# A block of two transformer layers on one core: wide and narrow matmuls in turns, and modulation columns in buffers of their own

## The chip, the cores and the metric

One core of a Trainium2 chip. TensorE (PE in the profile; PEld is its weight load), VectorE (DVE), ScalarE (ACT) and SyncE (SP, which only issues DMAs here) share one on-chip memory. The metric is the time of one execution on the device in microseconds (us), lower is better. A matmul here has a 128 x 128 weight tile and 512 ("wide") or 256 ("narrow") columns.

## What is computed

Two transformer blocks on x of 256 tokens by 2048 features, batch 1, in float32. Cut to what the change touches:

```python
def first_block(x, c, w_ada, b_ada, ...):
    mod = silu(c) @ w_ada + b_ada                   # 2048 -> 6 * 2048
    sh1, sc1, gt1, sh2, sc2, gt2 = split(mod, 6)
    h = rms_norm(x, g_mix) * (1 + sc1) + sh1
    z = h @ w_in            # q, k, v of two attentions, an indexer, two gates
    o_sb = stick_breaking_attention(...)            # 8 heads
    o_ds = indexer_sparse_attention(...)            # 8 heads, top 64 of 256 keys
    merged = sigmoid(gate_sb) * (o_sb @ w_o_sb) + sigmoid(gate_ds) * (o_ds @ w_o_dsa)
    x = x + gt1 * (merged @ w_out)
    h = rms_norm(x, g_ffn) * (1 + sc2) + sh2
    x = x + gt2 * ((silu(conv3(h @ w_gate)) * (h @ w_up)) @ w_down)
    return rms_norm(x, g_final)

def second_block(x, ...):     # gated linear attention, then a SwiGLU network
```

The second block has no modulation. Weights of all layers come from memory once, 583 MB in all.

## The kernel before

**Splitting.** Every weight tile of 128 x 1024 float32 (512 KB) is fetched by `weights` into a buffer `raw`, rounded by ACT into `hi` (L96), and DVE writes the rest, raw minus hi, into `lo` (L97). Activations are held as hi and lo halves too, side by side in a 512-column slot. A product is hi times (hi, lo) plus lo times hi. There are seven `raw`, four `hi` and four `lo` buffers, so the split runs up to four tiles ahead of PE.

**The matmul forms.** `dense_b` and `dense_wide` (most of the run) use a pair for each 128 x 128 tile: one wide matmul of `hi` with both halves (L114), then one narrow matmul of `lo` with the hi half (L115), both added into one accumulator bank. `mm3` (batches of the first projection, `dense_3`) uses three narrow ones (L124 to L126); `dense_a` uses three wide ones (L167 to L169), with the roles of weight and activation exchanged.

**Modulation.** Each of the 96 columns of `mod` is a 128 x 2048 slice (1 MB) of `w_ada`, multiplied with silu(c) and summed by DVE. `mod_fetch` takes two `raw` buffers for it, two DMAs of 512 KB (L201); `mod_reduce` does two DVE reductions of 1024 (L211), the second starting from the first's sum. The first 32 columns (shift and scale of the first norm) are needed one by one in `batch`, which runs the first projection for three groups of outputs over k = 0, 1, then 2 to 6, then 7 to 15. The other 64 are paced: `weights` adds `rate` to a credit at each tile and calls `mod_step` (reduce the oldest, then fetch the next) when it reaches one. 48 of them have to be there when `ffn` starts.

**The order of stages.** First projection (`batch`, to about 320 us), values of both attentions (`values`, `dense_a`), gate projections by `dense_3` with the attention's small steps taken from a list `bg` one per tile by `pump` (about 430 to 630 us), the two output projections, `w_out`, then the feed-forward network, the second block and its SwiGLU. A norm ends in `stat_end`: sums over features by PE, `keep_warm` (matmuls of ones whose result nobody reads), a square root.

**Who sets the order.** The program is written as one sequence; a scheduler orders each engine's instructions from the dependencies, the buffers and a priority (`high_priority(offset=120)` moves fetch and split ahead). All loads stand in SP's queue in one order: a load that waits for its buffer holds those behind it.

## Time and profile before

| what | value |
|---|---|
| median of 3 runs | 2732.74 us (2729.59 to 2732.83) |
| profiled execution | 2736.31 us |
| its span, first to last instruction | 2734.5 us, mean granted clock 0.997 |
| PE busy | 2684.6 us, 98% |
| DVE busy | 1879.9 us, 69% |
| ACT busy | 1299.8 us, 48% |
| read from memory | 579 MB, 213 GB/s over the span |

A busy PE says that matmuls follow one another, not that they follow at the smallest distance: matmul records overlap, and the distance from one start to the next is what counts. The granted clock is 1.00 at 2.4 GHz and 0.50 at 1.2 GHz.

### The profile page before, as it was taken

What the parts mean: (1) busy time and instruction counts of PE and PEld (TensorE: products, weight loads), DVE (VectorE), ACT (ScalarE), POOL (GpSimd) and SP (SyncE); (2) the same over time, 40 slices, a digit from 0 to 9 for tenths busy, and PEclk for the clock granted to TensorE, in tenths of its full rate; (3) what the DMA queues carried; (4) which work ended last, traced back from release to release, by engine and by line L of the source; (5) the groups of instructions that cost most, each with busy time, mean ns of one, the idle gap of its engine ahead of it and who ended that gap; (6) DMA issues with size and microseconds to landing.
All of it is one profiled execution on the core that took longest, in us unless ns stands there. A gap on an engine that the chain in (4) does not pass through costs nothing.

```text
span 2734.5 us, 42023 instructions
## 1 busy us (share of the span) xinstructions
PE 2684.6 (98%) x16364; PEld 2375.6 (87%) x16364; DVE 1879.9 (69%) x2892; ACT 1299.8 (48%) x1925; POOL 0.2 (0%) x4
## 2 busy tenths in 40 slices
PE   8999998999989999999999999999999999999999
PEld 7999878999878888888888888888888888888888
DVE  7997686667888777766555578467766666665544
ACT  5343344554445444444444465455544444444333
POOL 0000000000000000000000000000000000000000
PEclk9999999999999999999999999999999999999999
DMA  9998778678767666655666545545555555556664
GB/s 338 333 358 292 265 234 295 223 245 283 264 226 231 219 232 224 225 186 185 181 185 189 189 137 147 167 148 186 191 175 187 186 185 186 187 187 184 196 193 124
DMA packets 167681, 585.71 MB, mean 214 GB/s; under 512 B 18583, under 2 KB 23415, under 8 KB 167481
## 3 DMA queue, kind: packets, MB, share of 16 engines
q1 hardware_dynamic: 167482, 583.03, 65.0%
q8 instruction: 128, 2.10, 0.3%
q14 instruction: 71, 0.58, 0.1%
HBM read 579.22 MB, written 3.67 MB: 213 GB/s over the span
## 4 chain that ended last, share of the span: by engine, by line
PE 79%; DVE 5%; DMA 5%; issue 1%; ACT 0%; SPq 0%; DVEq 0%; ACTq 0%
PE acc L114 43%; PE acc L115 22%; DMA raw<-in_w_ada 3%; DVE lo L97 3%; PE acc L125 2%; PE acc L124 2%; PE acc L126 2%; PE acc L167 1%; PE acc L168 1%; PE acc L169 1%; PE misc L868 1%; PE acc L149 1%; DMA skew<-t 1%; DVE raw L211 0%; DMA raw<-in_w_in_b 0%
## 5 line engine op out<-in xcount | busy, mean ns | idle before, releaser
L114 PE MATMUL acc<-slot,hi 128*128 128x512 f32 x5024 | 1777.5, 397 | 0.0
L97 DVE TENSOR_TENSOR lo<-raw,hi 128x1024 fp32r<-128x1024 f32 (+1 forms) x916 | 1101.4, 1205 | 653.1 <-ACT hi L96 652.1
L96 ACT CAST hi<-raw 128x1024 fp32r<-128x1024 f32 (+1 forms) x916 | 946.1, 1034 | 1191.0 <-issue 483.7
L115 PE MATMUL acc<-slot,lo 128*128 128x256 f32 x5024 | 1415.7, 282 | 6.8 <-DVE lo L97 6.8
L114 PEld LDWEIGHTS acc<-slot,hi 128*128 128x128 f32 x5024 | 943.2, 188 | 231.5 <-issue 1.5
L115 PEld LDWEIGHTS acc<-slot,lo 128*128 128x128 f32 x5024 | 947.0, 188 | 9.7 <-DVE lo L97 8.7
L124 PE MATMUL acc<-slot,hi 128*128 128x256 f32 x1056 | 301.3, 286 | 6.5 <-ACT hi L96 3.5
L126 PE MATMUL acc<-slot,lo 128*128 128x256 f32 x1056 | 297.7, 284 | 8.7 <-DVE lo L97 8.7
L125 PE MATMUL acc<-slot,hi 128*128 128x256 f32 x1056 | 297.6, 283 | 0.0
L126 PEld LDWEIGHTS acc<-slot,lo 128*128 128x128 f32 x1056 | 200.0, 190 | 10.7 <-DVE lo L97 10.6
L124 PEld LDWEIGHTS acc<-slot,hi 128*128 128x128 f32 x1056 | 200.4, 190 | 8.2 <-ACT hi L96 4.5
L125 PEld LDWEIGHTS acc<-slot,hi 128*128 128x128 f32 x1056 | 200.7, 190 | 0.0
L211 DVE CUSTOM_DVE_ANT_0 raw<-raw,big,vecs 128x1024 f32<-128x1024 f32 x96 | 123.0, 1282 | 101.5 <-DMA raw<-in_w_ada 101.3
L211 DVE CUSTOM_DVE_ANT_0 raw<-raw,big,mod 128x1024 f32<-128x1024 f32 x96 | 123.0, 1281 | 8.8 <-DMA raw<-in_w_ada 8.0
L124 PE MATMUL misc<-slot,hi 128*128 128x256 f32 x384 | 105.7, 284 | 1.8 <-ACT hi L96 1.4
L125 PE MATMUL misc<-slot,hi 128*128 128x256 f32 x384 | 105.0, 282 | 0.0
L167 PE MATMUL acc<-hi,slot 128*128 128x512 f32 x256 | 103.2, 403 | 1.4 <-DVE slot L578 1.4
L126 PE MATMUL misc<-slot,lo 128*128 128x256 f32 x384 | 97.5, 286 | 5.1 <-DVE lo L97 4.7
L168 PE MATMUL acc<-lo,slot 128*128 128x512 f32 x256 | 101.3, 396 | 0.0
L169 PE MATMUL acc<-hi,slot 128*128 128x512 f32 x256 | 101.2, 395 | 0.0
L179 DVE TENSOR_TENSOR t<-acc,t 128x256 f32<-128x256 f32 x188 | 78.6, 418 | 0.3
L178 ACT COPY t<-acc 128x256 f32<-128x256 f32 x209 | 76.3, 365 | 0.8 <-PE acc L150 0.8
(228 smaller groups left out, 1792.4 us busy)
## 6 DMA issues: line engine op xcount, KB each, us to landing
raw<-in_w_gu SPq DMA_DIRECT2D x344, 512.0 KB, 3.9
raw<-in_w_ada SPq DMA_DIRECT2D x192, 512.0 KB, 5.5
raw<-in_w_in_k SPq DMA_DIRECT2D x96, 512.0 KB, 5.8
raw<-in_w_down SPq DMA_DIRECT2D x80, 512.0 KB, 3.6
raw<-in_w_dn SPq DMA_DIRECT2D x80, 512.0 KB, 3.7
raw<-in_gla_b SPq DMA_DIRECT2D x66, 512.0 KB, 3.5
raw<-in_w_in_b SPq DMA_DIRECT2D x50, 512.0 KB, 5.4
raw<-in_w_in_a SPq DMA_DIRECT2D x32, 512.0 KB, 4.5
```

The lines of the kernel that those rows point to most:

```text
L96: self.mark = nc.scalar.copy(hi[:, :n], raw[:, :n])
L97: nc.vector.tensor_sub(lo[:, :n], raw[:, :n], hi[:, :n])
L114: nc.tensor.matmul(acc, hi[:, w], x, start=(k + j == 0), stop=False, skip_group_check=True)
L115: nc.tensor.matmul(acc[:, 1], lo[:, w], x[:, 0], start=False, stop=(k + j == kt - 1), skip_group_check=True)
L124: nc.tensor.matmul(out, hi, x[:, 0], start=first, stop=False, **mm)
L125: nc.tensor.matmul(out, hi, x[:, 1], start=False, stop=False, **mm)
L126: nc.tensor.matmul(out, lo, x[:, 0], start=False, stop=last, **mm)
L167: nc.tensor.matmul(o, hs[k][:, 0, tt], hi[:, w], start=(k == 0), stop=False)
L168: nc.tensor.matmul(o, hs[k][:, 0, tt], lo[:, w], start=False, stop=False)
L169: nc.tensor.matmul(o, hs[k][:, 1, tt], hi[:, w], start=False, stop=(k == KD - 1))
L179: nc.vector.tensor_add(out, acc[:, 0], t)
L211: nc.vector.tensor_tensor_reduce(out=raw, in0=raw, in1=self.c_act[:, hf * 1024:(hf + 1) * 1024], scale=1.0, scalar=init, op0=ALU.mult, op1 ...
```

## The change

- `tile_mm` takes the place of the pair in `dense_b` and `dense_wide`: in each four tiles the first two are wide then narrow, the other two narrow then wide.
- A column of `w_ada` is one DMA of 1 MB into a tile `col` with two buffers of its own, and one DVE reduction over 2048. `raw` has four buffers in place of seven, the small scratch `t1` six in place of seven.
- `mod_step` fetches first and reduces the column before, so a column is fetched one step ahead. `batch` fetches at other places, and takes columns while more than one is waiting.
- `rate` is set by stage: 0.25, 0.2, 0.15, 0.38, 0.33, 0.25 in place of 0.28 throughout.
- In the list `bg` the first sparse-attention head's second step comes after two empty entries, so two weight tiles (48 matmuls) later.
- `keep_warm` in `stat_end` has 20 matmuls in place of 12.

```diff
--- before.py
+++ after.py
@@ -64,7 +64,7 @@
 
     def scr(self, n):
         if n <= S:
-            return self.sp.tile([P, S], F32, name="t1", tag="t1", bufs=7)
+            return self.sp.tile([P, S], F32, name="t1", tag="t1", bufs=6)
         return self.sp.tile([P, 512], F32, name="t2", tag="t2", bufs=4)[:, :n]
 
     def acc(self):
@@ -84,7 +84,7 @@
 
 
     def raw(self):
-        return self.wp.tile([P, 1024], F32, name="raw", tag="raw", bufs=7)
+        return self.wp.tile([P, 1024], F32, name="raw", tag="raw", bufs=4)
 
     def weights(self, src, n):
         nc = self.nc
@@ -101,8 +101,21 @@
             self.mod_step()
         return hi, lo
 
+    def tile_mm(self, acc, hi, lo, x, j, first, last):
+
+        def wide(start, stop):
+            self.nc.tensor.matmul(acc, hi, x, start=start, stop=stop, skip_group_check=True)
+
+        def narrow(stop):
+            self.nc.tensor.matmul(acc[:, 1], lo, x[:, 0], start=False, stop=stop, skip_group_check=True)
+        if j % 4 < 2 or first:
+            wide(first, False)
+            narrow(last)
+        else:
+            narrow(False)
+            wide(False, last)
+
     def dense_b(self, src, kt, hs, evac, pump=0):
-        nc = self.nc
         acc = self.acc()
         k = 0
         while k < kt:
@@ -110,10 +123,7 @@
             hi, lo = self.weights(src[:, k * P:(k + kn) * P], kn * P)
             for j in range(kn):
                 w = slice(j * P, (j + 1) * P)
-                x = hs[k + j]
-                nc.tensor.matmul(acc, hi[:, w], x, start=(k + j == 0), stop=False, skip_group_check=True)
-                nc.tensor.matmul(acc[:, 1], lo[:, w], x[:, 0], start=False, stop=(k + j == kt - 1),
-                                 skip_group_check=True)
+                self.tile_mm(acc, hi[:, w], lo[:, w], hs[k + j], j, k + j == 0, k + j == kt - 1)
             k += kn
             self.pump(pump)
         evac(acc)
@@ -145,10 +155,7 @@
             for j in range(8):
                 k, acc = k0 + j // nn, accs[j % nn]
                 w = slice(j * P, (j + 1) * P)
-                x = hs[k]
-                nc.tensor.matmul(acc, hi[:, w], x, start=(k == 0), stop=False, skip_group_check=True)
-                nc.tensor.matmul(acc[:, 1], lo[:, w], x[:, 0], start=False, stop=(k == kt - 1),
-                                 skip_group_check=True)
+                self.tile_mm(acc, hi[:, w], lo[:, w], hs[k], j, k == 0, k == kt - 1)
             self.pump(pump)
         for acc, evac in zip(accs, evacs):
             evac(acc)
@@ -194,28 +201,23 @@
         if not self.modq:
             return
         ci, j = self.modq.popleft()
-        raws = []
         with self.tc.high_priority(offset=offset):
-            for hf in range(2):
-                raws.append(self.raw())
-                self.nc.sync.dma_start(raws[-1], self.ap["w_ada"][ci * KD + j, :, hf * 1024:(hf + 1) * 1024])
-        self.colq.append((ci, j, raws))
+            col = self.wp.tile([P, D], F32, name="col", tag="col", bufs=2)
+            self.nc.sync.dma_start(col, self.ap["w_ada"][ci * KD + j])
+        self.colq.append((ci, j, col))
 
     def mod_reduce(self):
-        nc = self.nc
-        ci, j, raws = self.colq.popleft()
+        ci, j, col = self.colq.popleft()
         n = ci * KD + j
-        m = self.mod[ci][:, j:j + 1]
-        for hf, raw in enumerate(raws):
-            init = m if hf else self.vec["b_ada"][:, n:n + 1]
-            nc.vector.tensor_tensor_reduce(out=raw, in0=raw, in1=self.c_act[:, hf * 1024:(hf + 1) * 1024], scale=1.0,
-                                           scalar=init, op0=ALU.mult, op1=ALU.add, accum_out=m)
+        self.nc.vector.tensor_tensor_reduce(out=col, in0=col, in1=self.c_act, scale=1.0,
+                                            scalar=self.vec["b_ada"][:, n:n + 1], op0=ALU.mult, op1=ALU.add,
+                                            accum_out=self.mod[ci][:, j:j + 1])
         return ci, j
 
     def mod_step(self):
-        if self.colq:
+        self.mod_fetch()
+        if self.colq and (len(self.colq) > 1 or not self.modq):
             self.mod_reduce()
-        self.mod_fetch()
 
 
     def stat_begin(self, two=False):
@@ -269,7 +271,7 @@
         r1, r2 = self.rs[:, :S], self.rs[:, S:]
         if not self.st_two:
             self.token_sums(m[:, :S], (self.st[:, :S], self.sq[:, :S]))
-            self.keep_warm(12)
+            self.keep_warm(20)
             self.free(self.st)
             self.rstd(r1, m[:, :S], D)
             return r1
@@ -564,11 +566,11 @@
                         w = slice(j * P, (j + 1) * P)
                         self.mm3(banks[n // 2][:, (n % 2) * S:(n % 2 + 1) * S], hi[:, w], lo[:, w], hs[k],
                                  k == k0 and n % 2 == 0, k == k1 - 1)
-                    if len(hss) < KD:
-                        for _ in range((0, 3)[half] if b == k == 0 else 1 - half):
+                    for _ in range((0, 2)[half] if b == k == 0 else 1 if k == 0 else half):
+                        while len(self.colq) > 1:
+                            column()
+                        if len(hss) < KD:
                             self.mod_fetch()
-                if len(hss) < KD:
-                    column()
             for n in range(KD):
                 o, sc = dst[b * KD + n]
                 a = banks[n // 2][:, (n % 2) * S:(n % 2 + 1) * S]
@@ -586,7 +588,7 @@
         with self.tc.issue_after(self.mark.ins):
             nc.scalar.preload_act_table_set("natural_log_exp_and_others")
         self.load_consts()
-        self.rate = 0.28
+        self.rate = 0.25
         self.modq.extend((ci, j) for ci in (2, 4, 3, 5) for j in range(KD))
         batch(1, 7, KD)
         batch(2, 7, KD)
@@ -618,10 +620,11 @@
                 out.append(v)
             return out
 
+        self.rate = 0.2
         self.dsv = values(0, 2)
         parts = [self.ds_head(h) for h in range(NH)]
-        self.bg.append(parts[0][0])
-        for h in range(NH):
+        self.bg.extend((parts[0][0], parts[1][0], lambda: None, lambda: None, parts[0][1]))
+        for h in range(1, NH):
             if h + 1 < NH:
                 self.bg.append(parts[h + 1][0])
             self.bg.append(parts[h][1])
@@ -635,7 +638,9 @@
         gates += [self.alloc() for _ in range(9)]
         for n in range(7, 2 * KD):
             o = gates[n % KD][:, S:] if n < KD else gates[n % KD][:, :S]
+            self.rate = 0.15 if n < 14 else 0.38
             self.dense_3(nxt(), KD, hs, to(o), 1)
+        self.rate = 0.33
         self.drain()
         for v in self.dsv + self.sbv:
             self.free(*v)
@@ -652,6 +657,7 @@
                     nc.scalar.activation(g, g, AF.Tanh, scale=0.5)
                 nc.vector.scalar_tensor_tensor(g, g, 1.0, a, op0=ALU.add, op1=ALU.mult)
             self.dense_3(ap["w_o_dsa"][n], NH, ods, gated)
+        self.rate = 0.25
         ms = []
         for n in range(KD):
             g, g2 = gates[n][:, :S], gates[n][:, S:]
```

How the built programs differ, at three places. PE in the first block's feed-forward network, one weight tile of eight 128 x 128 pieces (`acc` the accumulator, `slot` the activation, numbers count the tiles made). Before:

```order
L114 MATMUL acc_14759<-slot29_9661,hi_14784 128x512
L115 MATMUL acc_14759<-slot29_9661,lo_14785 128x256
L114 MATMUL acc_14759<-slot30_9772,hi_14784 128x512
L115 MATMUL acc_14759<-slot30_9772,lo_14785 128x256
L114 MATMUL acc_14759<-slot31_9877,hi_14784 128x512
L115 MATMUL acc_14759<-slot31_9877,lo_14785 128x256
L114 MATMUL acc_14759<-slot32_9988,hi_14784 128x512
L115 MATMUL acc_14759<-slot32_9988,lo_14785 128x256
```

and after, the same eight (lines L107 and L110 are `tile_mm`'s wide and narrow):

```order
L107 MATMUL acc_14479<-slot29_9409,hi_14504 128x512
L110 MATMUL acc_14479<-slot29_9409,lo_14505 128x256
L107 MATMUL acc_14479<-slot30_9514,hi_14504 128x512
L110 MATMUL acc_14479<-slot30_9514,lo_14505 128x256
L110 MATMUL acc_14479<-slot31_9622,lo_14505 128x256
L107 MATMUL acc_14479<-slot31_9622,hi_14504 128x512
L110 MATMUL acc_14479<-slot32_9727,lo_14505 128x256
L107 MATMUL acc_14479<-slot32_9727,hi_14504 128x512
```

Two narrow matmuls now follow one another once in four pieces, and two wide ones where the next four begin.

SP in the gate projections, weight tiles 150 to 158 of the program. Before:

```order
L201 DMA raw_5414<-in_w_ada 128x1024
L201 DMA raw_5416<-in_w_ada 128x1024
L93 DMA raw_5450<-in_w_in_b 128x1024
L93 DMA raw_5487<-in_w_in_b 128x1024
L93 DMA raw_5526<-in_w_in_b 128x1024
L201 DMA raw_5534<-in_w_ada 128x1024
L201 DMA raw_5536<-in_w_ada 128x1024
L93 DMA raw_5569<-in_w_in_b 128x1024
```

and after:

```order
L93 DMA raw_5253<-in_w_in_b 128x1024
L206 DMA col_6692<-in_w_ada 128x2048
L93 DMA raw_5289<-in_w_in_b 128x1024
L206 DMA col_6794<-in_w_ada 128x2048
L93 DMA raw_5330<-in_w_in_b 128x1024
L93 DMA raw_5367<-in_w_in_b 128x1024
L206 DMA col_6937<-in_w_ada 128x2048
L93 DMA raw_5409<-in_w_in_b 128x1024
L206 DMA col_7088<-in_w_ada 128x2048
```

A column stands after each 1.5 weight tiles, before after each 3.6. The numbers show that these columns were written much later in the program (6692 beside weights 5253): the scheduler moved them up, and the rates alone don't set their place. All 96 stand before the 210th weight tile in place of the 362nd; from the 139th to the 182nd there are 28, before 13.

SP at the start of the program, before:

```order
L320 DMA big_83<-in_c 1x2048
L509 DMA slot0_87<-in_x 128x512
L509 DMA slot1_88<-in_x 128x512
L509 DMA slot2_89<-in_x 128x512
L509 DMA slot3_90<-in_x 128x512
```

and after:

```order
L93 DMA raw_206<-in_w_in_k 128x1024
L93 DMA raw_236<-in_w_in_k 128x1024
L93 DMA raw_278<-in_w_in_k 128x1024
L322 DMA big_83<-in_c 1x2048
L511 DMA slot0_87<-in_x 128x512
```

Three weight tiles now stand ahead of c, x and the first columns.

## Rows read from the trace of the kernel before

**Rows 1.** The page's first part: busy time, share of the span, instructions.

```profile
PE 2684.6 (98%) x16364; PEld 2375.6 (87%) x16364; DVE 1879.9 (69%) x2892; ACT 1299.8 (48%) x1925; POOL 0.2 (0%) x4
```

**Rows 2.** Busy time by stretch; PEclk is the granted clock.

```profile
core 0: us, PE busy (x) PEld busy (x) DVE busy (x) ACT busy (x) POOL busy (x), PEclk, DMA share, GB/s
0.00:60.00 60.00, 47.20 (x281) 40.57 (x282) 47.85 (x76) 31.25 (x62) 0.20 (x4) 0.94 0.94 339
60.00:300.00 240.00, 232.78 (x1920) 228.35 (x1919) 208.38 (x322) 96.94 (x112) 0.00 (x0) 1.00 0.89 321
300.00:430.00 130.00, 125.50 (x657) 102.33 (x657) 97.84 (x181) 51.69 (x65) 0.00 (x0) 1.00 0.78 252
430.00:500.00 70.00, 63.42 (x487) 61.43 (x486) 51.46 (x116) 39.87 (x88) 0.00 (x0) 0.95 0.82 282
470.00:612.00 142.00, 141.34 (x1139) 138.73 (x1138) 98.45 (x158) 78.75 (x142) 0.00 (x0) 1.00 0.71 234
630.00:720.00 90.00, 84.98 (x655) 80.88 (x654) 72.32 (x118) 42.30 (x68) 0.00 (x0) 1.00 0.80 274
720.00:810.00 90.00, 80.27 (x470) 69.25 (x468) 71.50 (x108) 40.15 (x62) 0.00 (x0) 1.00 0.76 259
846.00:1556.00 710.00, 710.00 (x4021) 616.59 (x4020) 477.65 (x661) 340.57 (x488) 0.00 (x0) 1.00 0.64 204
1990.00:2734.00 744.00, 740.57 (x4192) 642.83 (x4191) 427.37 (x563) 330.18 (x460) 0.00 (x0) 1.00 0.58 182
```

**Rows 3.** PE in order of time at 1000 us: start, us, engine, line.

```profile
1000.14 0.39 PE L114 MATMUL acc<-slot,hi 128*128 128x512 f32 x1
1000.37 0.28 PE L115 MATMUL acc<-slot,lo 128*128 128x256 f32 x1
1000.48 0.40 PE L114 MATMUL acc<-slot,hi 128*128 128x512 f32 x1
1000.72 0.28 PE L115 MATMUL acc<-slot,lo 128*128 128x256 f32 x1
1000.84 0.39 PE L114 MATMUL acc<-slot,hi 128*128 128x512 f32 x1
```

**Rows 4.** PE in order of time, the first and last of twelve wides.

```profile
1976.15 0.39 PE L114 MATMUL acc<-slot,hi 128*128 128x512 f32 x1
...
1979.96 0.39 PE L114 MATMUL acc<-slot,hi 128*128 128x512 f32 x1
```

**Rows 5.** PE in order of time: ends of 19 wide steps, of 15 narrow.

```profile
381.53 0.39 PE L169 MATMUL acc<-hi,slot 128*128 128x512 f32 x1
...
385.96 0.39 PE L167 MATMUL acc<-hi,slot 128*128 128x512 f32 x1
...
582.19 0.28 PE L126 MATMUL acc<-slot,lo 128*128 128x256 f32 x1
...
583.97 0.28 PE L126 MATMUL acc<-slot,lo 128*128 128x256 f32 x1
```

**Rows 6.** PE in order of time, a transpose in the first sparse-attention head.

```profile
450.21 0.47 PE L443 MATMUL misc<-cst,t 128*128 128x128 f32 x1 [5.12 <-ACT t L437]
```

**Rows 7.** Waits from 630 to 810 us: in total, times, longest.

```profile
DVE raw L211 <- DMA raw<-in_w_ada: 35.2, 15, 4.5
PE acc L115 <- DVE lo L97: 6.8, 6, 1.7
```

**Rows 8.** DVE's groups by shape: count, busy us, mean ns of one.

```profile
L97 DVE TENSOR_TENSOR lo<-raw,hi 128x1024 fp32r<-128x1024 f32 x884 | 1079.3, 1223 | 629.6 <-ACT hi L96 628.7
L97 DVE TENSOR_TENSOR lo<-raw,hi 128x512 fp32r<-128x512 f32 x32 | 22.2, 692 | 23.5 <-ACT hi L96 23.5
```

**Rows 9.** Reductions of columns (L211) from 470 to 612 us: DVE busy.

```profile
470.00:612.00 142.00, 29.68 (x46) 1.00 0.71 234
```

**Rows 10.** PE around two norms' ends.

```profile
810.08 0.77 PE L149 MATMUL acc<-slot,hi 128*128 128x512 f32 x1 [2.37 <-DVE slot L299]
...
1981.29 2.84 PE L258 MATMUL misc<-ones 128*128 128x128 f32 x24
```

## The prediction

> **What bounds the kernel now.** I read the busy shares first, then busy time by stretch, then the order in time inside the stretches, then waits. PE is busy 98% of the span [rows 1], so at most 50 us of PE's time is idle, and the table by stretch shows where: 12.8 of 60 us at the start, 7.2 from 60 to 300, 4.5 to 430, 6.6 to 500, then 5.0 and 9.7 up to 810, and nothing in the 710 us from 846; the 3.4 us of the last stretch are the end of the run [rows 2]. So after 810 us only the distance between matmuls counts. There the starts show it: wide to narrow 0.23 us, narrow to wide 0.11, then 0.24 and 0.12, that is 0.70 us for two pairs, in which every second pair is the longer one [rows 3]. The count says the same for the whole stretches: 4021 matmuls in 710 us and 4192 in 740.6 are 353.2 and 353.3 ns for each pair [rows 2]. But just before 1980 us the same pairs of the same shapes start 3.81 us apart over eleven, 346.4 ns [rows 4]. The long pairs are thus no price of the shapes; PE stays in one of two rhythms.
>
> **The order in turns.** Nothing is added: as many wide and narrow matmuls, as many weight loads. In eight matmuls the neighbours wide-narrow and narrow-wide fall from four each to three each, and narrow-narrow and wide-wide come in once each. The trace has these two apart, in the kernel's other forms: wide after wide 4.43 us for 19 steps, 233.2 ns, narrow after narrow 1.78 for 15, 118.7 [rows 5], together 351.9. One end is therefore a pair of 351.9 ns, 1.4 less than now, if each matmul costs what it does in its pure stream. The other is 346.4, 6.9 less, if the reversal every two tiles keeps PE out of the long rhythm, which repeats every two tiles too. The two slow stretches hold (4021 + 4192) / 2 = 4106 pairs: 5.7 us by the first end, 28.3 by the second. No row lies nearer to one than to the other: the neighbours are mixed, as in [rows 4], but not alternating. I take the middle, **-17 us**. A loss isn't excluded (a long step at every wide would add about as much as the good end gives); no row shows two long ones in succession, so it only has a share in the slow case.
>
> A rule speaks against any gain here: the Trainium skill, "TensorE: Matmul & The Clock Gate", section "Back-to-back issue gap", gives a distance that depends on the matmul's column count alone (N / 2.4 + 2.5 ns). By it the order of the shapes changes nothing and this term is 0; a pair would cost 325 ns (an estimate from that page). Rows 3 and 4 disagree, since the same two counts stand 353 and 346 ns apart.
>
> **The waits before 810 us**, each with its bounds:
>
> 1. The transpose at 450 us waits 5.1 us for the softmax of the first head [rows 6]. Two empty entries put 48 narrow matmuls of 118.7 ns, 5.7 us, in between: the wait goes. Behind it the clock is at the half level for a time (0.95 over 70 us, 3.5 us lost, about 1 of it while PE stood) [rows 2]. **-7.5** (-5 to -8.5); late next is the next head's softmax, which had 6 us already.
> 2. From 720 to 810 us PE idles 9.7 us [rows 2]. DVE stands there for columns not yet landed (35.2 us in 15 waits from 630 on), and PE waits for the `lo` queued behind them [rows 7]. In the built program no column is left in this stretch. What remains is the norm's end, 2.4 us before 810.08 [rows 10] and 0.7 ahead of it. **-6.5** (-5 to -7.5).
> 3. From 630 to 720, 5.0 us idle for the same reason [rows 2, 7]; columns stay, at one in 2.7 tiles, but each is fetched two tiles before DVE reaches it, where before it stood right ahead of its reduction. Half goes: **-2.5** (-5 to +3).
> 4. From 300 to 430, 4.5 us idle, same reasoning, less certain: **-2** (-4.5 to +2).
> 5. From 60 to 300 DVE is busy 208 of 240 us and DMA 89% [rows 2]. Half the elements of a split cost 531 ns less [rows 8], so 1024 more elements cost 1.06 us; a column now costs 29.68 / 11.5 = 2.58 us [rows 9], two halves of 1.29, and then 1.29 + 1.06 = 2.35. That is 0.23 us for each of some 27 columns, 6 us of DVE time, of which PE sees what lies in its 7.2 us of idle time: **-3** (-7 to +3).
> 6. At the start 1.57 MB of weights stand ahead of x and the columns: at 339 GB/s [rows 2] 4.6 us later. Two splits of 1.2 us leave the way to the first matmul and are done early. **+2** (-3 to +6).
> 7. The gate projections pay. From 470 to 612 us, where PE idles 0.7 us, DVE is busy 98.5 of 142 us, 29.7 of it for 11.5 columns [rows 2, 9]. After, about 25 columns stand there: 98.5 - 29.7 + 25 x 2.35 = 127.5 us, 90%, with reductions twice as long in front of `lo` and of the attention's steps. At 87% the stretch from 60 to 300 idles 3% [rows 2], which would be 4 us here; DMA, at 234 GB/s for 22 MB of weights and 12 of columns, would come to about 335, near the 339 of the start. **+6** (0 to +15).
> 8. Eight more matmuls in `keep_warm`, 2.84 us for 24 [rows 10], so 0.95: at 810 us they lie inside the 2.4 us wait; at 1981 they stand ahead of PE's next weights and cost 0.9. Against that, up to 1.7 us of half clock after 810. **-0.5** (-1 to +1).
>
> A single set of four `raw` costs nothing that I see: while two columns were held, before had three. The later 12 columns that leave the feed-forward stage save no time, as PE idles nowhere there [rows 2].
>
> **Sum.** Waits: -7.5 - 6.5 - 2.5 - 2 - 3 + 2 + 6 - 0.5 = -14. With the turns -31. The profiled execution took 2736.3 us (span 2734.5), 3.6 above the median of the runs: 2705.3 there, **2702 us** as a median.
>
> **The rivals.**
>
> - *The fast rhythm everywhere.* The turns give 28 us, not 17: 2691. For it: with undisturbed alternation the rhythm stays for the whole of [rows 4]. Against: nothing shows what two alike in succession do to it.
> - *The order does nothing.* PE takes 353 ns for any order of the shapes, and only the waits remain, 2732.7 - 14 = 2719. (The rule of the Trainium skill's page above amounts to this case.) For it: the pure streams' 351.9 lies nearer to 353.3 than to 346.4. Against: two rhythms exist.
> - *Slower: DVE becomes the bound in the gate projections.* The spare time there is 142 - 127.5 = 14.5 us. If 25 reductions wait for their columns as they do after 630 us, 35.2 / 15 = 2.3 us each [rows 7], that is 59 us, so 44 late instead of 6: 2702 + 38 = 2740 with the turns' gain, 2757 without. All gains are eaten from about 2 us of waiting for each column. For it: DMA would run near its highest rate of this trace. Against: a lead of two tiles, 5.7 us of PE's time or more.
> - *The change doesn't do what it says:* the rates don't set the places of columns, since the scheduler moved them up. That is in terms 2, 3 and 7 already.
>
> **Chances.** Forecast 0.42 (its own range 2690 to 2714), fast rhythm 0.20, order without effect 0.27, slower 0.11. A measurement of this kernel can tell about 0.2% from no change, here 5.5 us: faster is below 2727.3. Forecast and fast rhythm lie there, of the third case three quarters to four fifths: 0.83. Same 0.07, the third case with its bounds added; slower 0.10. The range leaves out the slow case and the ends of the two outer ones: 2676 to 2730.
>
> **What would show it.** The starts of PE at 1000 us: 8 matmuls in 1.39 us if the fast rhythm holds, 1.40 by the middle, 1.41 if nothing changes. The stretch between the feed-forward network's first matmuls and the end shrinks by 5 to 28 us. No wait at the first transpose, and a granted clock of 1.00 near it. DVE waits for `w_ada` well under the 35 us of 630 to 810. DVE busy about 90% in the later gate projections, with PE idle under 10 us. The prediction is wrong if PE idles 30 us or more there, if the start loses more than 6, or if pairs in turns take longer than 353 ns.

## The result, and the profile after

Four runs of the changed kernel gave a median of 2700.07 us (2693.64 to 2703.8), against 2732.35 for the kernel before beside it: a ratio of 0.988, 95% interval 0.986 to 0.990. The change makes the kernel 1.2% faster, 32 us; 2702 was forecast. The profiled execution took 2693.64 us, the lowest of the four. Five more runs of the same kernel (a2, below) gave 2695.41 (2690.51 to 2701.49); all nine have a median of 2696.3. The executions thus lie 13 us apart, and that spread turned out to be the most instructive part.

The page's first part after the change, to be read beside [rows 1]:

```profile
PE 2657.6 (99%) x16396; PEld 2371.9 (88%) x16396; DVE 1867.3 (69%) x2700; ACT 1303.8 (48%) x1927; POOL 0.2 (0%) x4
```

Busy time by stretch after, the same stretches and columns as [rows 2]:

```profile
60.00:300.00 240.00, 235.73 (x1963) 233.13 (x1963) 214.69 (x269) 99.47 (x114) 0.00 (x0) 1.00 0.91 336
300.00:430.00 130.00, 130.00 (x703) 107.74 (x703) 111.24 (x176) 55.91 (x71) 0.00 (x0) 1.00 0.90 316
430.00:500.00 70.00, 65.40 (x505) 63.14 (x504) 57.23 (x108) 39.12 (x90) 0.00 (x0) 0.98 0.87 312
470.00:612.00 142.00, 136.75 (x1094) 133.31 (x1093) 118.34 (x153) 74.89 (x138) 0.00 (x0) 1.00 0.85 305
630.00:720.00 90.00, 89.34 (x676) 85.44 (x675) 78.28 (x116) 45.85 (x74) 0.00 (x0) 1.00 0.80 277
720.00:810.00 90.00, 89.36 (x540) 79.26 (x540) 64.53 (x99) 48.77 (x74) 0.00 (x0) 1.00 0.55 176
```

PE idles 0.7 and 0.6 us from 630 to 810 where it idled 5.0 and 9.7, nothing from 300 to 430 where it idled 4.5. The gate projections (470 to 612) go the other way: 0.7 us before, 5.3 now, with DVE at 118 of 142 us and DMA at 305 GB/s. What ends the waits there, PE first, then DVE (engine, instruction, releaser: us in total, times, longest), 430 to 640 us:

```profile
PE misc L452 <- ACT t L449: 4.6, 2, 2.9
PE misc L483 <- DVE t L481: 3.5, 3, 1.6
...
DVE col L212 <- DMA col<-in_w_ada: 34.8, 17, 5.1
```

The first head's transpose, which waited 5.1 us [rows 6], doesn't appear. In its place the next step of the same chain waits (L452, values times weights): the wait was shortened and moved. DVE stands 34.8 us in this stretch for columns that haven't landed; from 630 to 810, where it stood 35.2 us before [rows 7], it is 5.0 now. What such a column holds up shows inside the first head's softmax, on DVE in order of time:

```profile
436.20 2.35 DVE L212 CUSTOM_DVE_ANT_0 col<-col,big,vecs 128x2048 f32<-128x2048 f32 x1 [4.91 <-DMA col<-in_w_ada]
...
438.48 0.16 DVE L437 RECIPROCAL mx<-mx 128x2 f32<-128x2 f32 x1
```

ACT has the sums of the exponentials at 432.1 us; their reciprocal, 0.16 us of work, comes at 438.5, behind a column for which DVE stood 4.91 us.

PE in order of time at 1000 us, as in [rows 3]; x2 is two matmuls alike in succession:

```profile
999.53 0.39 PE L107 MATMUL acc<-slot,hi 128*128 128x512 f32 x1
999.76 0.28 PE L110 MATMUL acc<-slot,lo 128*128 128x256 f32 x1
999.88 0.62 PE L107 MATMUL acc<-slot,hi 128*128 128x512 f32 x2
1000.34 0.28 PE L110 MATMUL acc<-slot,lo 128*128 128x256 f32 x1
1000.46 0.39 PE L107 MATMUL acc<-slot,hi 128*128 128x512 f32 x1
1000.69 0.40 PE L110 MATMUL acc<-slot,lo 128*128 128x256 f32 x2
1000.92 0.39 PE L107 MATMUL acc<-slot,hi 128*128 128x512 f32 x1
```

From 999.53 to 1000.92 are four pairs, 1.39 us, 348 ns each; before it was 353. The prediction had set 1.39 for the fast rhythm and 1.40 for the middle; the count below places it between.

Where the time went, by the start of the same matmul in each trace (weight tiles of the first stages, then wide matmuls of `tile_mm`, counted from their first):

| from, to | before, us | after | after, second profile | forecast of the change |
|---|---|---|---|---|
| 0 to weight tile 24 | 102.0 | 102.1 | 100.7 | +2 (6) |
| tile 24 to 95 | 213.1 | 208.6 | 209.0 | -3 (5) |
| 95 to 96 (values) | 106.3 | 103.2 | 103.1 | -2 (4) |
| 96 to 108 (first head) | 50.5 | 43.4 | 44.3 | -7.5 (1) |
| 108 to 144 (gates) | 128.4 | 136.3 | 135.4 | +6 (7) |
| 144 to first wide | 102.0 | 98.6 | 98.2 | -2.5 (3) |
| first to 250th wide | 112.9 | 99.3 | 99.3 | -7 (2, 8), -1 of the turns |
| 250th to last wide | 1914.8 | 1896.0 | 1899.3 | -16 of the turns |

The sums are -42.5 and -40.7 where the prediction has -31 (before's profile lies 4 us above the median of its runs).

### The profile page after: what moved, and what is told of

It reads as the page before. It is cut to its first block, busy times and chain, and to the rows that moved or that the text cites. A ratio compares the mean times of both kernels' runs of the same rounds, so it can differ in the third digit from the quotient of the medians.

```text
span 2691.9 us, 41770 instructions
## 1 busy us (share of the span) xinstructions
PE 2657.6 (99%) x16396; PEld 2371.9 (88%) x16396; DVE 1867.3 (69%) x2700; ACT 1303.8 (48%) x1927; POOL 0.2 (0%) x4
## 4 chain that ended last, share of the span: by engine, by line
PE 88%; DMA 6%; DVE 3%; issue 2%; ACT 1%; SPq 0%; DVEq 0%; ACTq 0%
PE acc L107 45%; PE acc L110 23%; PE acc L136 2%; PE acc L135 2%; DMA col<-in_w_ada 2%; PE acc L134 2%; PE acc L174 2%; PE acc L175 2%; PE acc L176 2%; DVE lo L97 1%; DMA raw<-in_w_in_k 1%; PE misc L135 1%; PE misc L134 1%; PE misc L136 1%; PE misc L874 1%
## 5 line engine op out<-in xcount | busy, mean ns | idle before, releaser
L107 PE MATMUL acc<-slot,hi 128*128 128x512 f32 x5120 | 1697.1, 393 | 0.6 <-DVE slot L301 0.6
L110 PE MATMUL acc<-slot,lo 128*128 128x256 f32 x5120 | 1228.2, 281 | 0.1
L110 PEld LDWEIGHTS acc<-slot,lo 128*128 128x128 f32 x5120 | 960.6, 188 | 107.2 <-issue 0.8
L107 PEld LDWEIGHTS acc<-slot,hi 128*128 128x128 f32 x5120 | 875.4, 188 | 112.8 <-issue 2.3
L136 PE MATMUL acc<-slot,lo 128*128 128x256 f32 x1056 | 291.8, 284 | 1.6 <-DVE lo L97 1.4
L212 DVE CUSTOM_DVE_ANT_0 col<-col,big,vecs 128x2048 f32<-128x2048 f32 x96 | 225.5, 2349 | 51.7 <-DMA col<-in_w_ada 51.3
L134 PEld LDWEIGHTS acc<-slot,hi 128*128 128x128 f32 x1056 | 199.8, 190 | 8.2 <-ACT hi L96 4.1
L135 PEld LDWEIGHTS acc<-slot,hi 128*128 128x128 f32 x1056 | 200.9, 190 | 1.2 <-DVE slot L301 1.1
L136 PE MATMUL misc<-slot,lo 128*128 128x256 f32 x384 | 105.9, 283 | 0.3 <-DVE lo L97 0.3
L174 PE MATMUL acc<-hi,slot 128*128 128x512 f32 x256 | 103.2, 403 | 0.0
L134 PEld LDWEIGHTS misc<-slot,hi 128*128 128x128 f32 x384 | 73.0, 191 | 2.9 <-ACT hi L96 2.7
```

The source lines that it names most:

```text
L107: self.nc.tensor.matmul(acc, hi, x, start=start, stop=stop, skip_group_check=True)
L110: self.nc.tensor.matmul(acc[:, 1], lo, x[:, 0], start=False, stop=stop, skip_group_check=True)
L134: nc.tensor.matmul(out, hi, x[:, 0], start=first, stop=False, **mm)
L135: nc.tensor.matmul(out, hi, x[:, 1], start=False, stop=False, **mm)
L136: nc.tensor.matmul(out, lo, x[:, 0], start=False, stop=last, **mm)
L174: nc.tensor.matmul(o, hs[k][:, 0, tt], hi[:, w], start=(k == 0), stop=False)
```

## The experiments

Rhythms are told by a count that everyone can repeat: the busy time of PE from 850 to 1500 us and from 2000 to 2650, two stretches without a pause, divided by half the number of matmuls in them. Columns: stretch, its length, PE busy (matmuls), clock, DMA share, GB/s. The changed kernel, first profile:

```profile
850.00:1500.00 650.00, 650.00 (x3735) 1.00 0.59 189
2000.00:2650.00 650.00, 650.00 (x3734) 1.00 0.60 191
```

650 / 3735 x 2 = 348.1 ns a pair. The kernel before gives 353.1 and 353.2. The count takes in the matmuls that lie across the edges and so reads up to 0.3 ns low; from the start of the first wide to that of the last, all stretches of plain alternation below give 346.7 or 353.3 ns, and all of turns of two 348.3 or 350.0, each to within 0.1.

### The turns: undone, alone, and the same program twice

Undone (e1 and, the same kernel once more, a3):

```
-        if j % 4 < 2 or first:
+        if True:
```

> The changed kernel with the order inside a tile as before (wide, then narrow, always); the columns, buffers and schedule stay as changed. My theory: the turns give 17 to 20 us, since in the traces a pair took 353.2 ns before and takes 348.4 ns in turns, over 4106 pairs, and the schedule gives the other 12 to 15; so 2718 to 2722 us here, with a pair at 353 ns in the long stretches. Rival, the order does nothing and the shorter pair comes with the new places of the columns: 2700 us and 348 ns. Rival, the turns are all of the gain: 2732.

2708.94 us (2695.49 to 2726.0, 12 runs), ratio to before 0.993 (0.990 to 0.996). The median fits no theory well, and the profiled execution (2695.49) shows why: plain alternation, at the short pair through both stretches.

```profile
850.00:1500.00 650.00, 650.00 (x3752) 1.00 0.59 189
2000.00:2650.00 650.00, 650.00 (x3752) 1.00 0.60 192
```

346.5 ns: not the turns' 348.1, and 6.6 below the 353 of the same order in the kernel before. So it seems that the time of plain alternation isn't a number but one of two; executions of this one program lie 30 us apart. Running this program and the changed one again tests it.

> The changed kernel with plain alternation (wide, then narrow) once more, the same as the earlier run of it, for a second profile of the same program. My theory: single executions from 2695 to 2726 again, and a profile in which at least one of the two long stretches runs at 353.3 ns a pair where the earlier profile had 346.7 in both; each long stretch at the slow rhythm costs 13 to 14 us (2050 pairs by 6.6 ns). Median 2705 to 2715. Rival, the rhythm belongs to the program: 346.7 ns in both again, and the spread has another cause.

2719.27 us (2716.67 to 2724.3, 8 runs). The second profile of the same program (2720.52 us):

```profile
850.00:1500.00 650.00, 650.00 (x3681) 1.00 0.58 186
2000.00:2650.00 650.00, 650.00 (x3681) 1.00 0.58 188
```

353.2 ns in both. Same instructions in the same order, same clock, 25 us apart; 4106 pairs x 6.7 ns are 27.5. So the program by itself doesn't set the rhythm. The two profiles are of two chips, but the chip alone doesn't set it either: e10 below has both cases on one chip, and the kernel before has both rhythms in one execution (346 ns ahead of 1980 us [rows 4], 353 in the stretches on either side). And since the kernel before took 2732.37 us beside a3, with plain alternation in both, the new schedule without the turns gives 13 us; the prediction has -14.

> The changed kernel once more, unchanged, beside the next run on the same chip. My theory now: with wide and narrow in plain alternation PE falls into a rhythm of 346.7 or of 353.3 ns a pair, which differs from one execution to the next and holds through a stretch of 700 us; in turns it has no such choice, or a smaller one (348.4 and 350.0 ns were both seen). So 2698 to 2703 us here, the runs within some 10 us. Rival, the spread comes from elsewhere (transfers): runs spread as widely as with the order undone, some 30 us.

2695.41 us (2690.51 to 2701.49, 5 runs), on the same chip as a3, so there the turns gave 24 us; between e1 and the changed kernel's first runs it was 9. The turns have a choice too, but a narrower one:

```profile
850.00:1500.00 650.00, 650.00 (x3717) 1.00 0.58 187
2000.00:2650.00 650.00, 650.00 (x3735) 1.00 0.59 191
```

349.7 in the first stretch, 348.1 in the second: 1.6 ns apart, up to 7 us over 4106 pairs.

The turns alone, on the kernel before (e2: `tile_mm` and its two calls, nothing else of the change):

> The kernel before with the turns alone; columns, buffers and schedule as before. My theory: 353.2 - 348.4 = 4.8 ns a pair over 4106 pairs is 20 us, so 2711 to 2715, and the waits before 810 us stay as they were (5 us at the transpose near 450 us). Rival, the order does nothing by itself: 2732. Rival, the two parts need each other (PE that runs faster meets the waits for columns earlier and gives part back): 2715 to 2725.

2717.9 us (2714.17 to 2721.15, 12 runs), ratio 0.996 (0.994 to 0.998): 15 us less than before (2732.57). The order has its gain without the new schedule. Its profile has 349.7 and 349.8 ns (3717 and 3716 matmuls); 3.4 x 4106 = 14 us. The median lies above my theory's range and in that of the rival by which PE gives part back at the waits. The trace decides against that rival: everything up to the 250th wide takes 807.8 us, against 815.2 before, so nothing is given back there. The theory's range was too low because it took 348.4 ns for both stretches, and the stretches ran at the slower of the turns' two values.

Where one rhythm goes over into the other shows in e1, at 819 us:

```profile
818.63 0.39 PE L107 MATMUL acc<-slot,hi 128*128 128x512 f32 x1
...
818.86 0.28 PE L110 MATMUL acc<-slot,lo 128*128 128x256 f32 x1
...
818.98 0.40 PE L107 MATMUL acc<-slot,hi 128*128 128x512 f32 x1
...
819.22 0.28 PE L110 MATMUL acc<-slot,lo 128*128 128x256 f32 x1
...
819.41 0.19 PEld L107 LDWEIGHTS acc<-slot,hi 128*128 128x128 f32 x1 [0.24 <-DVE t L186]
819.41 0.50 PE L107 MATMUL acc<-slot,hi 128*128 128x512 f32 x1
...
819.75 0.28 PE L110 MATMUL acc<-slot,lo 128*128 128x256 f32 x1
...
819.87 0.39 PE L107 MATMUL acc<-slot,hi 128*128 128x512 f32 x1
...
820.10 0.28 PE L110 MATMUL acc<-slot,lo 128*128 128x256 f32 x1
```

Until 819.22 the steps are 0.23, 0.12, 0.24, the long rhythm of [rows 3]. One weight load waits 0.24 us for a free accumulator, and from there every wide takes 0.23: the short rhythm holds to the end of the stretch, 700 us later. So PE can go from one into the other at a wait of a fraction of a microsecond. It need not: a3 has the same wait at the same place,

```profile
815.10 0.19 PEld L107 LDWEIGHTS acc<-slot,hi 128*128 128x128 f32 x1 [0.24 <-DVE t L186]
```

and is in the long rhythm before and behind it (3681 matmuls from 850 us on, above); e10 stays in the long one too. Why PE lands in one or the other isn't shown.

### Turns of other lengths

```
-        if j % 4 < 2 or first:
+        if j % 2 < 1 or first:      (e3)
+        if j % 8 < 4 or first:      (e4)
```

> The changed kernel with turns of one tile: wide narrow, narrow wide, so that the engine sees wide wide narrow narrow. Neighbours: one each of wide-wide, wide-narrow, narrow-narrow, narrow-wide in four matmuls. If a pair's time is the sum of what the kinds of neighbours cost: in turns of two the trace has the mixed steps at 235, 117, 231, 117 and so on, and the step of two wides at 228, that of two narrows at 122; each step comes out at its first matmul's time, so 348 ns and 2700 us again. If the long rhythm, which repeats every two tiles in the kernel before, is what a reversal breaks: reversing more often keeps it off at least as well, 346.5 to 348.4 ns, 2692 to 2700. Rival, the pure streams' 351.9 ns is what alike neighbours cost: 351 ns, 2710 us.

2710.21 us (2705.62 to 2713.22, 8 runs), 351.2 ns in both stretches. My two theories fall, and the rival, that alike neighbours cost what they cost in the pure streams, fits with its 351 ns and 2710 us. First stretch:

```profile
850.00:1500.00 650.00, 650.00 (x3702) 1.00 0.58 187
```

> The changed kernel with turns of four tiles (of a block of eight, four begin with the wide, four with the narrow). If a reversal costs nothing and only breaks a rhythm that would set in by itself after some tiles: between 348.4 ns and 353.3, 2700 to 2720 us. If the rhythm sets in only after many tiles and each reversal costs a little: below 348.4, down to 347.5, 2696. Rival, the order does nothing: 2700.

2701.0 us (2697.29 to 2712.72, 6 runs), 349.1 ns, inside the first theory's bounds.

```profile
850.00:1500.00 650.00, 650.00 (x3724) 1.00 0.59 188
```

Each is one profile, and a second might show another rhythm, as it did for turns of two. What is shown is that more reversals aren't better: 351.2 with one in every tile, 349.1 with one in four, 348.1 or 349.8 with one in two. A sum over kinds of neighbours doesn't give these.

### The two empty entries

```
-        self.bg.extend((parts[0][0], parts[1][0], lambda: None, lambda: None, parts[0][1]))
+        self.bg.extend((parts[0][0], parts[1][0], parts[0][1]))
```

> The changed kernel without the two empty entries in front of the first head's transposes. My theory, as in the prediction: the transpose waits for the softmax of the first head again, 5 us or more, and the clock falls to the half level behind it: 7.5 us slower (5 to 8.5) than with the entries, about 2707. In the trace of the changed kernel that transpose still waits 3.07 us at 445 us and the clock still falls; so a rival: the entries moved the wait less than I thought, 3 us slower, 2703. A second rival: the softmax is late by a fixed time whatever stands ahead, no change, 2700.

2705.57 us (2700.56 to 2706.51, 6 runs), 10 us more than the changed kernel on the same chip (2695.41). The profiles say less: from weight tile 96 to 144 it takes 183.0 us instead of 179.7, so 3.3, and even that isn't clear: the seven profiles that have the entries and unpinned columns take 177.4 to 184.1 us there (e6 and e1 at the ends). Its long stretches ran at 349.8 ns both, the other's at 349.7 and 348.1, and that is 3.4 us of chance. PE's waits from 430 to 640 us:

```profile
PE misc L483 <- DVE t L481: 5.9, 4, 2.7
PE misc L445 <- ACT t L439: 4.7, 1, 4.7
PE misc L452 <- ACT t L449: 0.8, 1, 0.8
```

The transpose waits 4.7 us again, and L452 only 0.8. (With the entries, the wait at 445 us is L452's, 2.90 us; the expectation takes it for the transpose's.) The entries move the wait from one step of the chain to the next; that they also take off a part isn't shown beyond the spread. The mechanism of 7.5 us isn't borne out by the profile; by the times alone it couldn't be told. Here too DVE stands for a column inside the first head's softmax, for 4.12 us.

### Columns held where the rates put them

Each column's fetch is ordered behind the transfer of the weight tile it belongs to, its reduction behind that tile's `lo`; the scheduler can't move them up any more (e7, and e11 the same again). The edit, cut; `self.dma` and `self.sub` are that transfer and that `lo`:

```
+        with self.tc.issue_after(self.dma.ins):
             self.mod_fetch()
         if self.colq and (len(self.colq) > 1 or not self.modq):
+            with self.tc.issue_after(self.sub.ins):
                 self.mod_reduce()
```

> The changed kernel with each modulation column held behind the weight tile that the rate puts it at (its fetch behind that tile's transfer, its reduction behind that tile's lo), so that the scheduler can't pull columns forward into the gate projections. At the start the constants and x also stand ahead of the weights. My theory: the gate projections have one column in 2.7 tiles instead of nearly one a tile, and get their 8 us back; the columns land in the feed-forward network, where nothing idles for them: 2692 to 2695. Rival: the columns that stay for the stretches from 630 us on make DVE wait there again, as before the change (7 to 9 us lost from 630 to 810): 2699 to 2702. Rival, slower: more than 2703, if the reductions behind lo keep the next lo waiting.

(The trace shows that three weight tiles still stand ahead of x at the start, other than this says.) 2687.42 us (2682.27 to 2689.52, 5 runs), ratio 0.983 (0.981 to 0.985), 8 us less than the changed kernel on the same chip. The stretches, for [rows 2] and the same of the changed kernel above:

```profile
430.00:500.00 70.00, 69.96 (x554) 67.71 (x553) 51.26 (x103) 43.49 (x96) 0.00 (x0) 1.00 0.72 253
470.00:612.00 142.00, 141.99 (x1148) 139.61 (x1147) 105.17 (x139) 78.89 (x139) 0.00 (x0) 1.00 0.77 270
630.00:720.00 90.00, 90.00 (x663) 85.54 (x662) 79.40 (x114) 47.80 (x76) 0.00 (x0) 1.00 0.80 285
720.00:810.00 90.00, 89.42 (x540) 79.25 (x539) 80.11 (x120) 51.51 (x79) 0.00 (x0) 1.00 0.73 254
```

All waits of PE from 300 to 2690 us:

```profile
PE acc L107 <- DVE slot L303: 0.6, 1, 0.6
```

The gate projections lose nothing, and neither do the stretches behind them, though more columns stand there; the rival falls. The wait at L452 is gone as well, without any edit to the attention: that chain goes through DVE, and DVE stood for columns. The first head's reciprocal now waits for ACT alone:

```profile
436.09 0.17 DVE L439 RECIPROCAL mx<-mx 128x2 f32<-128x2 f32 x1 [0.86 <-ACT t L438]
```

From tile 96 to 144 it takes 168.9 us, the same in all four profiles with pinned columns, against 179.7 (and 178.9 before the change). So what was left of term 1's wait and the loss of term 7 had one cause: late columns in DVE's queue. The empty entries stand in e7 too, and no run pins the columns without them.

> The kernel with pinned columns once more, beside the next three on the same chip. 2682 to 2690 us again, median 2686; 348.4 or 350.0 ns a pair in each long stretch, not always the one that the first profile had there.

2686.62 us (2685.79 to 2688.01, 4 runs); 349.7 and 349.8 ns, where e7 had 348.2 and 349.8.

> Pinned columns, with plain alternation (wide, then narrow) in place of the turns. My theory: a pair takes 346.7 or 353.3 ns by execution and stretch; both long stretches fast would be 2687 - 2050 x 2.5 ns x 2 = 2677, both slow 2687 + 2050 x 4.1 ns x 2 = 2704; the median lies at the slow end, 2700 to 2708, since 27 of 38 runs of the kernel before and 12 of 20 of the changed one with plain alternation lie there or near. The turns are then worth 15 to 20 us on this schedule too. Rival: the schedule without late columns leaves PE in the fast rhythm, 2677, and the turns cost 10 us.

Four runs lie from 2703.05 to 2706.48 and two at 2674.30 and 2674.53, with nothing between (median 2703.22). The forecast of 2704 with both stretches slow and 2677 with both fast is what came. The profiled one (2705.26) is at 353.2 ns twice. The turns' 2687 lies between the two: 17 us under the usual case of plain alternation, 12 over its good one; over the mean of these six (2694.5) they gain 8.

### The start

All weight tiles behind the constants, x and two columns, with pinned columns (pin_x). The edit, cut; `self.first` is the second column's fetch:

```
+            with self.tc.issue_after(self.first.ins):
                 self.dma = nc.sync.dma_start(raw[:, :n], src)
```

> Pinned columns, and at the start all weight tiles behind the constants, x and the first two columns (the change had put three weight tiles ahead of them). My theory: the start is limited by what all of these move together, since in the traces before and after the change the 24th weight tile's matmuls begin at 102.0 and 102.1 us although the first begin at 20.3 and 25.1: no difference beyond 2 us from the pinned kernel. The prediction had put the change's order there at +2 us, so 2 us faster by it: 2684. Rival: the first weights arrive late and the start loses 3 us: 2690.

2682.31 us (2677.01 to 2683.17, 4 runs), 4 us less than e11 on the same chip; ratio to before 0.982 (0.980 to 0.983). It has the best median of all. The first 60 us, e11:

```profile
0.00:60.00 60.00, 45.00 (x284) 38.78 (x284) 46.93 (x57) 32.51 (x64) 0.20 (x4) 0.97 0.91 332
```

and pin_x:

```profile
0.00:60.00 60.00, 47.34 (x300) 39.92 (x301) 49.15 (x60) 34.51 (x69) 0.20 (x4) 1.00 0.94 352
```

PE works 2.3 us more, weight tile 24 begins at 97.8 us instead of 100.1 (99.8 to 102.1 in all profiles of the change's order), and the granted clock is 1.00 instead of 0.97, which is part of it. The wait for `c` falls from 7.3 us to 2.6. The prediction's +2 for this term is what undoing it returns; my later reading, that it is worth nothing, was wrong.

### The warming matmuls

```
-            self.keep_warm(20)
+            self.keep_warm(12)
```

> The changed kernel with the last norm's row of warming matmuls at 12, as before the change, in place of 20. The prediction put the eight more at -0.5 us. In the trace of the changed kernel PE waits 0.58 us behind them at 787.9 us and the clock stays whole; before the change it waited 2.37 us and ran 3.4 us at half clock. My theory now: with 12 the wait grows by the 0.9 us taken out, and the clock falls behind it, 1.7 us: 1 to 2 us slower, too little for the times, to be read from the profile. Rival: the clock holds over the longer wait, and nothing changes (0.9 us less of matmuls, 0.9 more of waiting).

2701.01 us (2698.24 to 2705.92, 4 runs). PE at the norm's end in the changed kernel:

```profile
783.54 3.73 PE L260 MATMUL misc<-ones 128*128 128x128 f32 x32
787.86 0.47 PE L107 MATMUL acc<-slot,hi 128*128 128x512 f32 x1 [0.58 <-DVE slot L301]
```

and with 12:

```profile
786.80 1.95 PE L260 MATMUL misc<-ones 128*128 128x128 f32 x16
791.11 0.47 PE L107 MATMUL acc<-slot,hi 128*128 128x512 f32 x1 [2.37 <-DVE slot L301]
```

The wait is 2.37 us, to the hundredth that of [rows 10], and from the 200th wide to the 250th it takes 29.7 us as with 20 (29.6; 33.8 before the change). The next wides run at 0.39 us, no half clock. So the rival holds: the added matmuls fill a wait and give nothing. Before the change the clock did fall behind the same wait (0.63 us for a wide from 810.86 on). There PE had been busy for 80.3 of the 90 us ahead [rows 2], here for 87.6, but that isn't what decides: e2, with 12 too, has the same wait behind 80.8 busy us of 90, and its clock stays whole.

```profile
804.10 0.47 PE L107 MATMUL acc<-slot,hi 128*128 128x512 f32 x1 [2.37 <-DVE slot L306]
```

What does decide isn't shown.

## Why the prediction was right, and where it wasn't

- **The turns, -17: right in the sum, for a reason I had only half.** Measured: 5.0 ns a pair (348.1) or 3.4 (349.7) against 353.2, so 20 or 14 us, on both sides of my middle. That the middle came so near was luck: it was halfway between two ends, and PE runs at neither of them in turns. I had read the two rhythms as something that the order sets off; they are two states that an execution falls into, and the kernel before can have either: of its 53 runs 47 lie from 2726 to 2740 us and six from 2714 to 2720, about one stretch's 14 us lower (no trace of such a run was kept). The turns take the good case away with the bad one. The rival "the order does nothing" (2719) falls by e2: the same matmuls, 15 us. (The rule that the prediction names beside it doesn't hold here either: the runs show 346.5 to 353.2 ns for the same two column counts. The Trainium skill, "TensorE: Matmul & The Clock Gate", section "Back-to-back issue gap", gives that formula for an isolated matmul and says that in a stream the weight load sets the spacing too; the prediction left that out.)
- **The fast rhythm everywhere** (2691) isn't what the turns do; only plain alternation was seen at 346.5.
- **Term 1, the transpose, -7.5:** the stretch gave -7.1 and -6.2, but the step failed. I called the wait the softmax's and credited the empty entries; e5 puts them at 3.3 us in the profile, inside the spread, and e7 removes all of the wait that they had left. What made the softmax late was DVE's queue: in the changed kernel a column that landed 4.91 us late stood in front of its reciprocal. "Late next is the next head's softmax" was wrong as well: it was the same head's product.
- **Terms 2 and 8, -7 from 720 us to behind the norm:** -13.6, of which 1.2 are the turns. Mis-sized: I left 3.1 us of idle time there and 0.6 remained (9.1 gained in place of 6.5); the wait that stood from 702 to 720 us was counted to term 3; and the half clock behind 810 (1.7 us) went, though not by the eight matmuls: in e6 it stays away without them.
- **Term 3:** -3.4 and -3.8 with its part up to the first wide, for -2.5. **Term 4:** -3.1 for -2. **Term 5:** -4.5 and -4.1 for -3; it isn't shown, since e6 and e7, with the same weights there, took 215.3 and 213.8 us in place of 208.6, no less than the 213.1 before. Part of that is the clock, granted at 0.98 and 0.99 from 60 to 300 us instead of 1.00. All inside their bounds.
- **Term 6, the start, +2:** 0.1 and -1.3 in the two traces, where the gain of other edits may lie over it; undone it returned 2.3 us.
- **Term 7, the gates, +6:** +7.9 and +7.0. By its steps: 23 columns instead of 25 from 470 to 612 us, DVE 118 us instead of 127.5, DMA 305 GB/s instead of 335, PE idle 5.3 us. The price per column was right: the reductions alone (L212, two records a column) give 2.36 us each in the second row below, for 2.35 (in the first, from which the 23 are, the window cuts one off). The slower rival, where each column is waited for 2.3 us, has its mechanism (34.8 us in 17 waits of 2.0) but not its price: DVE had the room.

```profile
470.00:612.00 142.00, 53.13 (x46) 1.00 0.85 305
430.00:500.00 70.00, 25.92 (x22) 0.98 0.87 312
```

- **The sum:** -31 forecast, -42 between the two profiles, -32 and -37 between the medians (a2 beside its 2732.37). Terms 2, 5 and 8 were too small; that the median came out 2 us from the forecast was in part luck, since the first four runs of the changed kernel lay above the later five.

Still open: what decides which rhythm an execution falls into, why more runs of before than of e1 are in the long one (the share may differ by chip: the low runs of before are 5 of 25, 1 of 13 and 0 of 11 on the three chips of the experiments), and what else than the clock makes 60 to 300 us differ by 7 us between kernels that are alike there. No run undoes the new buffers, the single reduction or the rates one by one; what terms 2 to 5 gained is read from the traces and not shown by an experiment.

## What to carry to other kernels

Where PE never waits, look at the starts of the matmuls: a repeating extra of ten nanoseconds is a cost, and it can be a property of the execution, so take several profiles of one program before crediting an order of instructions. An order that narrows such a choice is worth its distance from the usual case, and costs the rarer good one. Where a scheduler may move a helper's work forward, pin it: an operation that waits for a transfer in an engine's queue delays all that stands behind it, and here that looked like a slow softmax.

## What the runs showed of the hardware

- The same stream of wide (128x512) and narrow (128x256) matmuls in alternation takes 346.5 or 353.2 ns a pair at a granted clock of 1.00; each holds for hundreds of microseconds. Behind the same wait of 0.24 us PE went from the long into the short in e1 and stayed in the long in a3.
- Orders with reversals have their own distances: 348.1 or 349.8 (every two tiles), 349.1 (four), 351.2 (each).
- The same 2.37 us wait was followed by 3.4 us of the half clock before the change, and by none in e2 and e6, in e2 after as busy a stretch.
- A reduction of 128x2048 took 2.36 us with its read-out, two of 128x1024 2.58 [rows 9].
- An operation on DVE that waited 4.91 us for its transfer held up a 0.16 us operation behind it whose input was there.
